# Seven products of quarters in place of eight: latent keys and six gate tiles of an attention encoder on one core

## The chip, the cores and the metric

The kernel runs on one core of a Trainium2 chip. A core has five engines with queues of their own: PE (matmuls; PEld is its weight load), DVE, ACT and POOL (elementwise work, of which POOL can't read the matmuls' accumulators in PSUM), and SP, which here only issues DMA transfers. The metric is device time in microseconds of one execution.

## The reference, cut to what matters

```python
def mla_mixer(h, w_in, q_norm, w_uq, kv_norm, w_ukv, w_out):
    proj = h @ w_in                       # h = rms_norm(x, g), 1024 x 1024
    c_q, c_kv, k_pe, gate = proj[..., :s1], proj[..., s1:s2], proj[..., s2:s3], proj[..., s3:]
    q = (rms_norm(c_q, q_norm) @ w_uq).reshape(B, L, MLA_HEADS, MLA_QK_DIM)
    kv = (rms_norm(c_kv, kv_norm) @ w_ukv).reshape(B, L, MLA_HEADS, QK_NOPE_DIM + V_HEAD_DIM)
    ...
    q_pe = apply_rope(q_pe, cos[:, None, :], sin[:, None, :])
    k_pe = apply_rope(k_pe, cos, sin)
    ...
    return (o * jax.nn.silu(gate)) @ w_out

h = x + mla_mixer(rms_norm(x, g), ...)    # DEPTH = 1: one layer
return rms_norm(h, final_norm)
```

With 1024 tokens and width 1024, `proj` has 384 columns of latent queries, 256 of latent keys and values ("latent keys" below), 64 of rotary key and 1024 of gate (8 heads of 128).

## The kernel before

All is float32, made from pairs: an operand is split into a high part of a shorter mantissa that PE multiplies fast and a low part (the rest), and `mm3` adds three products, high by high, high by low and low by high. `split` makes a high part on POOL and the low part on DVE. Activations lie transposed: `xh`, `xl` hold x times its gain, 8 blocks of 128 rows (k) by 1024 tokens. The norm's factor of each token (`rx`) is applied to results.

Stages, in the order of the program:

1. Latent queries (lines 161 to 192): for each k, x and a block of weights are loaded and split, and three output tiles of 128 x 1024 are accumulated, 144 matmuls of 512 columns. Copies put them into `craw[0]` to `craw[2]`.
2. The gate stage (lines 274 to 380). `stream(m)` computes one output tile of 128 x 1024: raw weights are loaded in two parts of 256 KB (`gwr`, two buffers), split into `gwh` and `gwl` (three buffers each), and 8 k by 2 halves by 3 make 48 matmuls. Tiles 3 and 4 are the latent keys, then come a rotary key (32 matmuls, lines 285 to 311), and eight gate tiles (`stream_gate`: a product with `rx_sb` on DVE, then Silu on ACT). `rstd_x` makes `rx` from rows of x; `latent_sums`, `latent_norm` and `latent_scale` normalise the latents; `cq_h`, `cq_l` are the split queries. Between gate tiles 1 to 4 `rope_half` computes rotary queries (18 matmuls a call), turns them with DVE, POOL and ACT in rooms of the home tiles (`craw_a`, `craw_b`) and sends the parts to a scratch tensor in memory, `qpe_d`.
3. Attention for 8 heads (lines 385 to 727), which reads `qpe_d` back, makes keys, queries and values of a head, scores, softmax, an exchange through DMA and the products with values; then the output projection and the last norm.

The order on each engine is planned when the program is built: the planner takes ready instructions by their place in the program's text (`later` moves that place), against a model of durations, and each engine then runs its list in order. A tile from a pool waits until the buffer's last reader is done; the pools of the gate stage close at line 382, and attention's pools take their memory.

Of the kernel before, what the change touches and what calls it, by code (L numbers as in the profile page):

```python
# [14 lines left out]
P = 128  # L15
# [14 lines left out]
def kernel(  # L30
# [19 lines left out]


    nc = tc.nc
    mm = nc.tensor.matmul

    def f32(ap):
        return ap.bitcast(F32)

    def mm3(ps, lh, ll, rh, rl, first, last):
        mm(ps, lhsT=lh, rhs=rh, start=first, stop=False)  # L59
        mm(ps, lhsT=lh, rhs=rl, start=False, stop=False)  # L60
        mm(ps, lhsT=ll, rhs=rh, start=False, stop=last)  # L61

# [55 lines left out]
    gp = xctx.enter_context(tc.tile_pool(name="gp", bufs=3, side="right"))  # L118
    rw = xctx.enter_context(tc.tile_pool(name="rw", bufs=2, side="right"))
    xp = xctx.enter_context(tc.tile_pool(name="xp", bufs=1, side="right"))  # L120
# [3 lines left out]
    def total(ssq, half, name):  # L124


        src = ssq[:, halves(half)]
        top = xs.tile([DR, HT], F32, name="ss_t")
        both = xs.tile([P, HT], F32R, name="ss_b")
        nc.scalar.copy(top, src[DR:P])  # L130
        nc.gpsimd.tensor_add(top, top, src[0:DR])
        nc.scalar.copy(both[0:DR], top)
        nc.vector.tensor_sub(both[DR:P], top, f32(both[0:DR]))
        ps = ps_t.tile([P, HT], F32, name=f"sum_{name}", tag="t")
        mm(ps, lhsT=ones, rhs=both, start=True, stop=True)
        return ps

    def rsqrt(v, s, r):
# [5 lines left out]
        nc.vector.scalar_tensor_tensor(r, s, 1.5, r, op0=ALU.add, op1=ALU.mult)  # L144

    with ExitStack() as wctx:
        wp = wctx.enter_context(tc.tile_pool(name="wp", bufs=3))

# [12 lines left out]
        for k in range(KD):  # L161
# [14 lines left out]
            for hs in [halves(0), halves(1)] if k < 3 else [slice(0, L)]:  # L176
                nc.scalar.activation(xh[:, k, hs], xr[:, hs], AF.Copy, scale=g_sb[:, k:k + 1])
                nc.vector.scalar_tensor_tensor(
                    xl[:, k, hs], xr[:, hs], g_sb[:, k:k + 1], f32(xh[:, k, hs]),
                    op0=ALU.mult, op1=ALU.subtract,  # L180
                )
            units = [(m, half) for half in range(2) for m in range(3)]
            if k == KD - 1:
# [9 lines left out]

    gpool = ctx.enter_context(tc.tile_pool(name="gate", bufs=1))
    gate = gpool.tile([P, H, L], F32, name="gate")
    cctx = ExitStack()
    wts = cctx.enter_context(tc.tile_pool(name="wts", bufs=1))
    kvp = cctx.enter_context(tc.tile_pool(name="kvp", bufs=1))
    kv_h = kvp.tile([P, 2, L], F32R, name="kv_h")
    kv_l = kvp.tile([P, 2, L], F32R, name="kv_l")  # L200
    rx_sb = xs.tile([P, L], F32, name="rx_sb")
# [10 lines left out]

    def rstd_x():

        rows = x.rearrange("(p j) c -> p j c", j=KD)
        for j in range(KD):
            xn = home[1][:, 1 + j % 3]
            nc.sync.dma_start(xn, rows[:, j])
            nc.scalar.activation(xn, xn, AF.Square, accum_out=ssx[:, j:j + 1])
        nc.vector.tensor_scalar(v_s, ssx, 1.0 / D, EPS, op0=ALU.mult, op1=ALU.add)  # L220
        rsqrt(v_s, s_s, rx)
        nc.vector.tensor_mul(mx, rx, rx)
        spread("rx", rx, rx_sb)

    def latent_sums(ms, name):
        cs, sq = gate[:, 4], gate[:, 5]
        for i, m in enumerate(ms):
            if i == 0:
                nc.scalar.activation(cs, craw[m], AF.Square)
            else:  # L230
                nc.scalar.activation(sq, craw[m], AF.Square)
                nc.gpsimd.tensor_add(cs, cs, sq)
        line = gate[0:1, 6]
# [17 lines left out]

    def stream(m):
        wh, wl = [], []
        for kq in range(2):
            wh.append(gp.tile([P, 4, P], F32R, name=f"gwh_{m}_{kq}", tag="gwh"))
            wl.append(gp.tile([P, 4, P], F32R, name=f"gwl_{m}_{kq}", tag="gwl"))
            wr = gp.tile([P, 4, P], F32, name=f"gwr_{m}_{kq}", tag="gwr", bufs=2)
            nc.sync.dma_start(wr, wg[m - 3 - (m > 5), :, kq * 4:(kq + 1) * 4])
            split(wr, wh[-1], wl[-1])
        ps = wide(f"g_{m}")  # L260
        for k in range(KD):
            for half in range(2):
                hs = halves(half)
                mm3(ps[:, hs], wh[k // 4][:, k % 4], wl[k // 4][:, k % 4], xh[:, k, hs], xl[:, k, hs],
                    k == 0, k == KD - 1)
        return ps

    def stream_gate(i):
        ps = stream(6 + i)
        gt = gate[:, i]  # L270
        nc.vector.tensor_mul(gt, ps, rx_sb)
        nc.scalar.activation(gt, gt, AF.Silu)

    rstd_x()
    ps = stream(3)
    nc.scalar.copy(craw[3], ps)
    latent_sums((0, 1, 2), "sq")
    ps = stream(4)
    nc.scalar.copy(craw[4], ps)
    latent_norm("sq", QR, "rq", gate[:, 7])  # L280
    latent_sums((3, 4), "sk")

    wr = gp.tile([P, KD, DR], F32, name="wpe_r", tag="gwr", bufs=2)
    nc.sync.dma_start(wr, wpe)
# [4 lines left out]
    for k in range(KD):  # L291
        w = w_pe[k // 4][:, k % 4].rearrange("p a b -> p (a b)")
        for half in range(2):
            hs = halves(half)
            mm(ps[:, hs], lhsT=w, rhs=xh[:, k, hs], start=k == 0, stop=False)
            mm(ps[:, hs], lhsT=w, rhs=xl[:, k, hs], start=False, stop=k == KD - 1)
    rk_sb = gate[0:DR, 1:3]
    nc.sync.dma_start(rk_sb, rope_k)
    kp = home[1][:, 3]
    nc.vector.tensor_mul(kp, ps, rx_sb)  # L300
    kr = gate[:, 3]
# [10 lines left out]

    latent_scale((0, 1, 2), gate[:, 7])
    latent_norm("sk", KR, "rk", gate[:, 7])
    cqp = cctx.enter_context(tc.tile_pool(name="cqp", bufs=1))
    cq_h = [cqp.tile([P, L], F32R, name=f"cq_h{m}") for m in range(3)]
    cq_l = [cqp.tile([P, L], F32R, name=f"cq_l{m}") for m in range(3)]
    for m in range(3):
        nc.scalar.copy(cq_h[m], craw[m])
        nc.vector.tensor_sub(cq_l[m], craw[m], f32(cq_h[m]))  # L320
    stream_gate(0)
    def load_split(shape, src, tag, bufs, pool=None, raw=None):
# [3 lines left out]
        wr = (raw or wts).tile(shape, F32, name=f"{tag}_r", tag="w_r")  # L326
        nc.sync.dma_start(wr, src)
        split(wr, wh, wl)
        return wh, wl

    def load_q(src, pool=None):
        return load_split([P, 3, P], src, "wq", 2, pool, pool)

    def load_k(h):
        return load_split([P, 2, P], wuk[h], "wk", 1)

# [4 lines left out]
    nc.sync.dma_start(rope_sb, rope_q.rearrange("c p t -> p c t"))  # L341
    rooms = [(home[0][:, 0], home[0][:, 1]), (home[0][:, 2], home[1][:, 3])]

    def rope_half(g, half, w):
# [3 lines left out]
        for i in range(2):  # L348
            ab.append(acc("ab"))
            for k in range(3):  # L350
                mm3(ab[i], w[i][0][:, k], w[i][1][:, k], cq_h[k][:, hs], cq_l[k][:, hs], k == 0, k == 2)
        cos, sin = rope_sb[:, 0, hs], rope_sb[:, 1, hs]
        for i, (f0, f1, op) in enumerate(((cos, sin, ALU.subtract), (sin, cos, ALU.add))):
            t, hl = rooms[((g * 2 + half) * 2 + i) % len(rooms)]
            t0, t1 = t[:, 0:HT], t[:, HT:L]
            hi, lo = hl[:, 0:HT], hl[:, HT:L]
            nc.vector.tensor_mul(t0, ab[0], f0)
            nc.vector.tensor_mul(t1, ab[1], f1)
            nc.gpsimd.tensor_tensor(t0, t0, t1, op=op)
            nc.scalar.copy(hi.bitcast(F32R), t0)  # L360
            nc.vector.tensor_sub(lo.bitcast(F32R), t0, hi)
            for c, src in ((i, hi), (2 + i, lo)):
                nc.sync.dma_start(qpe_d[g * 4:(g + 1) * 4, c, :, hs], src)

    w_rope = [[load_q(wqp[j], rw) for j in range(2)], None]
    for i in range(1, H):
        stream_gate(i)
        if i == 2:
            w_rope[1] = [load_q(wqp[2 + j]) for j in range(2)]
        if i == 5:  # L370
            latent_scale((3, 4), gate[:, 7])
        if i == 6:
            for m in range(2):
                nc.gpsimd.tensor_scalar(kv_h[:, m], craw[3 + m], 1.0, 1.0, op0=ALU.mult, op1=ALU.mult)
                nc.vector.tensor_sub(kv_l[:, m], craw[3 + m], f32(kv_h[:, m]))
# [430 lines left out]
```

## Time and profile before

| | |
|---|---|
| median of 3 runs | 587.53 us (587.33 to 588.08) |
| profiled execution | 587.4 us |
| its span, first to last instruction | 585.7 us |
| mean granted clock of PE | 0.993 |
| matmuls in the profile | 2604 |

The page gives for each engine its busy time, for slices of the span the busy share, and for groups of equal instructions the number, mean duration and what the engine waited for. Windows give the same for a chosen stretch; the timeline gives the single instructions with start and duration in us. Durations of matmuls overlap, so their spacing is read from starts.

### The profile page before, as it was taken

How to read it: one execution, taken by the hardware profiler on the slowest of the kernel's cores; microseconds unless marked ns; L12 is line 12 of the kernel's file. 1: busy time of each engine (PE TensorE's matmuls, PEld its weight loads, DVE VectorE, ACT ScalarE, POOL GpSimd, SP SyncE). 2: the span in 40 equal slices, each digit the busy share in tenths (PEclk: the TensorE clock that was granted, in tenths of full speed). 3: DMA queues.
4: the chain of work that ended last, by engine and by line, in shares of the span. 5: the costliest groups of instructions: out<-in, count | busy, mean ns of one | idle time of the engine just before them, and what ended most of it. 6: DMA issues, size and time to landing. Idle time of an engine off the chain costs nothing.

```text
span 585.7 us, 7657 instructions
## 1 busy us (share of the span) xinstructions
PE 571.8 (98%) x2604; PEld 472.8 (81%) x2604; DVE 425.4 (73%) x573; ACT 275.5 (47%) x438; POOL 233.8 (40%) x201
## 2 busy tenths in 40 slices
PE   9999999999999999999999999999999979999995
PEld 5888888888888878888888888888888858788885
DVE  4923589475236799988888988898888894984663
ACT  4348463021014455553655455645365662644652
POOL 1623512343102345643553535533434874683000
PEclk9999999999999999999999999999999979999999
DMA  8766221324211448674457464763476458521332
GB/s 263 275 206 245 95 74 38 124 93 141 109 38 46 94 117 193 154 171 109 107 132 179 105 153 109 168 148 94 100 162 147 132 135 213 198 77 54 138 132 107
DMA packets 35962, 78.66 MB, mean 134 GB/s; under 512 B 7314, under 2 KB 11154, under 8 KB 35860
## 3 DMA queue, kind: packets, MB, share of 16 engines
q1 hardware_dynamic: 34628, 76.21, 48.3%
q10 hardware_dynamic: 1296, 1.97, 0.9%
q8 instruction: 20, 0.33, 0.2%
q14 instruction: 18, 0.15, 0.1%
HBM read 36.19 MB, written 8.41 MB: 76 GB/s over the span
## 4 chain that ended last, share of the span: by engine, by line
PE 90%; SPq 3%; DVE 2%; ACT 1%; DMA 1%; issue 1%; POOL 0%; DVEq 0%; ACTq 0%; POOLq 0%
PE g L59 6%; PE g L61 6%; PE g L60 6%; PE o L59 5%; PE o L60 5%; PE o L61 5%; PE pv L60 5%; PE pv L59 5%; PE pv L61 5%; PE s L59 4%; PE s L60 4%; PE s L459 4%; PE s L61 4%; PE s L458 4%; SPq L481 3%; PE q L59 2%
## 5 line engine op out<-in xcount | busy, mean ns | idle before, releaser
L472 POOL TENSOR_SCALAR probs<-probs,rc 128x1024 f32<-128x1024 f32 x64 | 84.3, 1319 | 113.0 <-DVE rc L471 108.9
L466 ACT ACTIVATE probs<-s,nmx 128x1024 f32<-128x1024 f32 x64 | 71.6, 1118 | 113.3 <-DVE nmx L464 110.4
L473 DVE STREAM_TRANSPOSE probs<-probs 128x1024 f32<-128x1024 f32 x64 | 79.2, 1238 | 15.8 <-POOL probs L472 14.2
L464 DVE TENSOR_REDUCE nmx<-s 128x1 f32<-128x1024 f32 x64 | 76.0, 1207 | 3.8 <-PE s L459 3.7
L488 ACT CAST pt_h<-d 128x1024 fp32r<-128x1024 f32 x64 | 65.3, 1052 | 8.0 <-PE pv L61 4.9
L59 PE MATMUL g<-xh,gwh 128*128 128x512 f32 x160 | 62.2, 389 | 0.0
L60 PE MATMUL g<-xl,gwh 128*128 128x512 f32 x160 | 62.2, 389 | 0.0
L61 PE MATMUL g<-xh,gwl 128*128 128x512 f32 x160 | 62.2, 389 | 0.0
L493 POOL TENSOR_TENSOR pt_l<-d,pt_h 128x512 fp32r<-128x512 f32 x32 | 49.1, 1534 | 26.0 <-ACT pt_h L488 25.3
L60 PE MATMUL pv<-pt_l,v_h 128*128 128x512 f32 x128 | 50.3, 393 | 2.4 <-POOL pt_l L493 2.0
L59 PE MATMUL s<-k_h,q_h 128*128 128x512 f32 x128 | 50.2, 392 | 1.2 <-ACT probs L466 1.2
L490 DVE TENSOR_TENSOR pt_l<-d,pt_h 128x1024 fp32r<-128x1024 f32 x32 | 48.8, 1524 | 3.5 <-ACT pt_h L488 3.3
L59 PE MATMUL pv<-pt_h,v_h 128*128 128x512 f32 x128 | 50.1, 392 | 0.0
L60 PE MATMUL s<-k_l,q_h 128*128 128x512 f32 x128 | 49.9, 390 | 0.0
L61 PE MATMUL pv<-pt_h,v_l 128*128 128x512 f32 x128 | 49.9, 389 | 0.0
L61 PE MATMUL s<-k_h,q_l 128*128 128x512 f32 x128 | 49.9, 389 | 0.0
L458 PE MATMUL s<-kk_h,qpe 128*128 128x512 f32 x128 | 49.8, 389 | 0.0
L459 PE MATMUL s<-kk_l,qpe 128*128 128x512 f32 x128 | 49.8, 389 | 0.0
L59 PE MATMUL o<-woh,o_split 128*128 128x512 f32 (+1 forms) x118 | 45.8, 388 | 2.5 <-ACT o_split L575 2.5
L60 PE MATMUL o<-wol,o_split 128*128 128x512 f32 (+1 forms) x118 | 45.6, 386 | 0.0
L61 PE MATMUL o<-woh,o_split 128*128 128x512 f32 (+1 forms) x118 | 44.5, 383 | 0.0
L576 DVE TENSOR_TENSOR o_split<-gate,o_split 128x512 fp32r<-128x512 f32 (+2 forms) x48 | 32.5, 708 | 9.4 <-ACT o_split L575 9.3
(194 smaller groups left out, 1237.1 us busy)
## 6 DMA issues: line engine op xcount, KB each, us to landing
d<-probs SPq DMA_DIRECT2D x256, 128.0 KB
gwr<-in_wg SPq DMA_DIRECT2D x20, 256.0 KB
craw_b<-in_x SPq DMA_DIRECT2D x8, 512.0 KB
qpe<-qpe_d SPq DMA_DIRECT2D x16, 256.0 KB
wor<-in_wo SPq DMA_DIRECT2D x16, 256.0 KB
xr<-in_x SPq DMA_DIRECT2D x16, 256.0 KB
xr<-in_xT SPq DMA_DIRECT2D x5, 512.0 KB
qpe_d<-craw_a SPq DMA_DIRECT2D x8, 256.0 KB
```

The lines of the kernel that those rows point to most:

```text
L59: mm(ps, lhsT=lh, rhs=rh, start=first, stop=False)
L60: mm(ps, lhsT=lh, rhs=rl, start=False, stop=False)
L61: mm(ps, lhsT=ll, rhs=rh, start=False, stop=last)
L458: mm(s[:, ks], lhsT=qpe_s, rhs=kk_h[:, ks], start=False, stop=False)
L459: mm(s[:, ks], lhsT=qpe_s, rhs=kk_l[:, ks], start=False, stop=True)
L464: maxima[u] = nc.vector.tensor_reduce(nmx, s, axis=AX.X, op=ALU.max, negate=True)
L466: exps[u] = nc.scalar.activation(p_t.rearrange("p j k c -> p k j c"), s.rearrange("p (k j c) -> p k j c", k=8, j=4), AF.Exp, bias=nmx, acc ...
L472: nc.gpsimd.tensor_scalar(p_t, p_t, rc, 1.0, op0=ALU.mult, op1=ALU.mult)
L473: nc.vector.transpose(out=p_t, in_=p_t)
L488: nc.scalar.copy(hi, src)
L490: nc.vector.tensor_sub(lo, src, f32(hi))
L493: nc.gpsimd.tensor_sub(lo[:, 2:4], src[:, 2:4], f32(hi[:, 2:4]))
```

## The change

Each of four pairs of output tiles (latent keys 3 and 4; gates 0 and 4, 1 and 5, 2 and 6) becomes a product of two 2 x 2 matrices of quarters: weights of tile a and of tile b, each for k 0 to 3 and 4 to 7, against x's four quarters `x11`, `x12`, `x21`, `x22` (k half by token half). It is computed by seven products with sums of quarters in front and behind: `t1` to `t4` are four sums of x's quarters, made once and split (`combine_x`; the first differences in the loop of stage 1; `t3` is written over `x12`, which `restore_x12` loads and splits again afterwards), and each pair makes four sums of weights and seven sums of results on DVE (`pair_start`, `pair_end`). A product is 4 k by 3 = 12 matmuls.

High parts of the gate weights are made by ACT instead of POOL; the latent sums by DVE instead of POOL. Raw weights have seven buffers instead of two. Gates 3 and 7 are computed as before, each in two halves, between the four rotary products (`gate_half`), and the rotary parts lie in `gwr`'s buffers instead of the home tiles. The rotary key's product comes right after the start of the first pair and is copied out at once. Several helpers are placed behind a given instruction (`issue_after`).

```diff
+            if k < 4:
+                nc.vector.tensor_sub(raw_a[:, k], xr[:, halves(1)], xr[:, halves(0)])
+                split_gained(raw_a[:, k], k, t1)
...
+    def combine_x():
+        for k in range(4):
+            nc.vector.scalar_tensor_tensor(
+                raw_a[:, k], raw_a[:, k], g_sb[:, k:k + 1], f32(x22[0][:, k]), op0=ALU.mult, op1=ALU.subtract
+            )
+        nc.vector.tensor_sub(raw_a, raw_a, f32(x22[1]))
+        split_act(raw_a, t2)
+        nc.vector.tensor_add(raw_b, raw_a, f32(x11[0]))
+        nc.vector.tensor_add(raw_b, raw_b, f32(x11[1]))
+        split_act(raw_b, t3)
+        nc.vector.tensor_add(raw_a, raw_a, f32(x21[0]))
+        nc.vector.tensor_add(raw_a, raw_a, f32(x21[1]))
+        return split_act(raw_a, t4)
+
+    def g_parts(src, shape=(P, 4, P)):
+        wh = gp.tile(list(shape), F32R, name="gwh", tag="gwh")
+        wl = gp.tile(list(shape), F32R, name="gwl", tag="gwl")
+        split_act(src, (wh, wl))
+        return wh, wl
...
+    def pair_start(a, b, dst_a, dst_b):
+
+        r11, r12 = g_load(a, 0), g_load(a, 1)
+        ps = wide("g")
+        p1, p2 = ps[:, 0:HT], ps[:, HT:L]
+        product(p1, g_parts(r11), x11)
+        nc.scalar.copy(dst_a[:, 0:HT], p1)
+        product(p2, g_parts(r12), x21)
+        return a, b, dst_a, dst_b, r11, r12, p2
+
+    def pair_end(state):
+        a, b, dst_a, dst_b, r11, r12, p2 = state
+        (c11, c12), (c21, c22) = ((d[:, 0:HT], d[:, HT:L]) for d in (dst_a, dst_b))
+        r21, r22 = g_load(b, 0), g_load(b, 1)
+        s = gp.tile([P, 4, P], F32, name=f"gws_{a}", tag="gwr", bufs=7)
+        nc.vector.tensor_add(s, r21, r22)
+        p5 = acc("g")
+        product(p5, g_parts(s), t1)
+        nc.vector.tensor_sub(s, r11, s)
+        p6 = ps_t.tile([P, HT], F32, name="g", tag="t")
+        product(p6, g_parts(s), t2)
+        nc.vector.tensor_add(c12, p6, c11)
+        nc.vector.tensor_add(c11, p2, c11)
+        nc.vector.tensor_sub(r21, r21, r11)
+        p7 = acc("g")
+        middle = product(p7, g_parts(r21), t3)
+        added = nc.vector.tensor_add(c21, p7, c12)
+        nc.vector.tensor_add(c22, p5, c21)
+        nc.vector.tensor_add(c12, p5, c12)
+        nc.vector.tensor_add(s, r12, s)
+        p3 = ps_t.tile([P, HT], F32, name="g", tag="t")
+        product(p3, g_parts(s), x22)
+        nc.vector.tensor_add(c12, p3, c12)
+        p4 = acc("g")
+        last = product(p4, g_parts(r22), t4)
+        nc.vector.tensor_add(c21, p4, c21)
+        return middle, added, last
...
+    pairs = [gate_start(0)]
+    combined = combine_x()
+    pair_end(first)
+    squares_x()
+    with tc.issue_after(combined.ins):
+        norm_x()
+    pairs.append(gate_start(1))
+    bounds = pair_end(pairs[0])
+    with tc.issue_after(bounds[0].ins):
+        latent_sums((0, 1, 2), "sq")
+    gate_end(0)
+    pairs.append(gate_start(2))
...
+    restore_x12()
+    direct = {"raw": [g_load(5, j) for j in range(2)]}
+    w_rope = [load_q(None, load_early([P, 3, P], wqp[j])) for j in range(2)]
+    gate_half(3, 0, direct)
+    direct["raw"] = [g_load(9, j) for j in range(2)]
+    raw_rope = [load_early([P, 3, P], wqp[2 + j]) for j in range(2)]
...
+    rope_half(0, 0, w_rope)
+    gate_half(3, 1, direct)
+    rope_half(0, 1, w_rope)
+    w_rope = [load_q(None, raw) for raw in raw_rope]
+    gate_half(7, 0, direct)
+    w_k = load_k(0, load_early([P, 2, P], wuk[0]))
+    latent_scale((3, 4), gate[:, 7])
...
+    rope_half(1, 0, w_rope)
+    gate_half(7, 1, direct)
+    rope_half(1, 1, w_rope)
```

More of the change, by code (lines that the diff above doesn't have):

```diff
@@ L60, in mm3 @@
         mm(ps, lhsT=lh, rhs=rl, start=False, stop=False)
-        mm(ps, lhsT=ll, rhs=rh, start=False, stop=last)
+        return mm(ps, lhsT=ll, rhs=rh, start=False, stop=last)
     def split(raw, hi, lo):
@@ L192 @@
         nc.vector.tensor_copy(craw[2][:, HT:L], a_5)
[L194 to L200, printed above, removed]
+    t2, t4 = t_parts("t2", "t4")
     rx_sb = xs.tile([P, L], F32, name="rx_sb")
@@ L268, in stream_gate, with split_act @@
[L268 to L285, printed above, removed]
+    def split_act(src, hl):
+        hi, lo = hl
+        nc.scalar.copy(hi, src)
+        return nc.vector.tensor_sub(lo, src, f32(hi))
@@ new lines, in g_parts, with g_load, product @@
+    def g_parts(src, shape=(P, 4, P)):
[3 more added lines that the diff above has]
+        return wh, wl
+    def g_load(w, j):
+        raw = gp.tile([P, 4, P], F32, name=f"gwr_{w}_{j}", tag="gwr", bufs=7)
+        nc.sync.dma_start(raw, wg[w, :, 4 * j:4 * j + 4])
+        return raw
+    def product(ps, w, x_part):
+        for k in range(4):
+            last = mm3(ps, w[0][:, k], w[1][:, k], x_part[0][:, k], x_part[1][:, k], k == 0, k == 3)
+        return last
@@ new lines, in gate_end, with gate_start, restore_x12 @@
+    def gate_end(i):
+        for j in (i, 4 + i):
+            nc.vector.tensor_mul(gate[:, j], gate[:, j], rx_sb)
+            nc.scalar.activation(gate[:, j], gate[:, j], AF.Silu)
+    def gate_start(i):
+        return pair_start(2 + i, 6 + i, gate[:, i], gate[:, 4 + i])
+    def restore_x12():
+        for k in range(4):
+            raw = gp.tile([P, HT], F32, name=f"xr2_{k}", tag="gwr", bufs=7)
+            nc.sync.dma_start(raw, xT[k * P:(k + 1) * P, halves(1)])
+            split_gained(raw, k, x12)
@@ new lines, in gate_half @@
+    def gate_half(i, half, state):
+        if half == 0:
+            state[i] = wide("g"), [g_parts(raw) for raw in state.pop("raw")]
+        ps, w = state[i]
+        hs = halves(half)
+        for k in range(KD):
+            mm3(ps[:, hs], w[k // 4][0][:, k % 4], w[k // 4][1][:, k % 4], xh[:, k, hs], xl[:, k, hs],
+                k == 0, k == KD - 1)
+        if half:
+            nc.vector.tensor_mul(gate[:, i], ps, rx_sb)
+            nc.scalar.activation(gate[:, i], gate[:, i], AF.Silu)
@@ L286 @@
+    first = pair_start(0, 1, craw[3], craw[4])
+    wr = gp.tile([P, KD, DR], F32, name="wpe_r", tag="gwr", bufs=7)
     nc.sync.dma_start(wr, wpe)
@@ L311 @@
         nc.vector.tensor_sub(kk_l[d], kp[0:DR], f32(kk_h[0:DR]))
-    latent_scale((0, 1, 2), gate[:, 7])
+    latent_norm("sq", QR, "rq", home[1][:, 3])
+    bounds = pair_end(pairs[1])
+    with tc.issue_after(bounds[2].ins):
+        latent_sums((3, 4), "sk")
+    gate_end(1)
+    bounds = pair_end(pairs[2])
+    with tc.issue_after(bounds[1].ins):
+        latent_scale((0, 1, 2), home[1][:, 3])
     latent_norm("sk", KR, "rk", gate[:, 7])
+    gate_end(2)
+    tctx.close()
+    cctx = ExitStack()
     cqp = cctx.enter_context(tc.tile_pool(name="cqp", bufs=1))
@@ L348, in rope_half @@
         for i in range(2):
-            ab.append(acc("ab"))
+            ab.append(acc("ab") if half == 0 else ps_t.tile([P, HT], F32, name="ab", tag="t"))
             for k in range(3):
```

104 lines of the change are left out of this document (53 added, 51 removed).

## The prediction

> **What bounds the kernel now.** I read the page's busy shares, its slices and its chain first. In the slices each digit is a fortieth of the span.
>
> ```profile
> span 585.7 us, 7657 instructions
> PE 571.8 (98%) x2604; PEld 472.8 (81%) x2604; DVE 425.4 (73%) x573; ACT 275.5 (47%) x438; POOL 233.8 (40%) x201
> PE   9999999999999999999999999999999979999995
> DVE  4923589475236799988888988898888894984663
> PE 90%; SPq 3%; DVE 2%; ACT 1%; DMA 1%; issue 1%; POOL 0%; DVEq 0%; ACTq 0%; POOLq 0%
> ```
>
> TensorE (PE) is busy 98% of the span and holds 90% of the chain, so a matmul removed is time removed as long as nothing else makes PE wait. VectorE (DVE) is half free in slices 3 to 12, the gate stage, and nearly full afterwards. Next I read the windows of the gate stage, and the first matmul of it, of the stage after it and of the scores.
>
> ```profile
> 37.90:171.40 133.50, 133.50 (x590) 110.35 (x589) 69.95 (x94) 49.10 (x66) 41.56 (x37) 1.00 0.33 110
> 37.92 0.39 PE L59 MATMUL g<-xh,gwh 128*128 128x512 f32 x1
> 171.36 0.39 PE L59 MATMUL k<-kv_h,wk_h 128*128 128x512 f32 x1
> 179.62 0.39 PE L59 MATMUL s<-k_h,q_h 128*128 128x512 f32 x1
> ```
>
> The columns after the stretch are its length, then busy us (and instructions) of PE, weight loads, DVE, ACT and POOL, the granted clock, the DMA share and GB/s. PE has no gap in 133.5 us; 590 matmuls make 0.2263 us each (the 389 ns means of the page overlap). DVE works 70 us of these 133.5, ACT 49, POOL 42. In the slices PE stays at 9 or more through the stages on both sides.
>
> **The change, part by part.** *Matmuls.* A pair of output tiles took 2 x 48; now it takes 7 products of 4 x 3 = 84. Four pairs (latent keys, gates 0/4, 1/5, 2/6) save 48 matmuls: 48 x 0.2263 = 10.9 us. The two direct gates, the rotary key (32) and the rotary products (72) keep their count. That is the whole gain, and all of it lies on the path. The stage would end at 171.4 - 10.9 = 160.5.
>
> *What pays for it.* Almost every added operation is DVE's, so I price DVE by spacing, from start to start where operations follow one another:
>
> ```profile
> 118.20 1.28 DVE L357 TENSOR_TENSOR craw_a<-ab,craw_b 128x512 f32<-128x512 f32 x2
> 119.40 1.27 DVE L358 TENSOR_TENSOR craw_a<-ab,craw_b 128x512 f32<-128x512 f32 x2
> 85.39 3.48 DVE L320 TENSOR_TENSOR cq_l<-craw_a,cq_h 128x1024 fp32r<-128x1024 f32 x3
> 88.80 2.76 DVE L311 TENSOR_TENSOR kk_l<-craw_b,kk_h 64x1024 fp32r<-64x1024 f32 x2
> 25.86 1.15 ACT L177 ACTIVATE xh<-xr,g_sb 128x1024 fp32r<-128x1024 f32 x1 [2.51 <-DMA xr<-in_xT]
> 29.07 1.27 DVE L178 SCALAR_TENSOR_TENSOR xl<-xr,g_sb,xh 128x1024 fp32r<-128x1024 f32 x1
> 36.76 1.23 DVE L190 COPY craw_a<-s_b 128x1024 f32<-128x1024 f32 x1 [4.63 <-PE s_b L61]
> 38.12 0.69 DVE L192 COPY craw_a<-acc 128x512 f32<-128x512 f32 x1
> 56.11 0.42 DVE L65 TENSOR_TENSOR wpe<-wpe_r,wpe 128x256 fp32r<-128x256 f32 x1
> 55.63 0.17 DVE L143 TENSOR_TENSOR small<-small 128x8 f32<-128x8 f32 x1
> 55.83 0.17 DVE L144 SCALAR_TENSOR_TENSOR small<-small 128x8 f32<-128x8 f32 x1
> ```
>
> Two 512-wide operations take 1.20 us (118.20 to 119.40): 0.60 each. Three 1024-wide ones take 3.41: 1.14 each. A 2048-wide one, which the trace lacks, is then 0.60 + 3 x 0.54 = 2.22 by the same slope (its bounds: two of 1024, 2.28, and four times 0.54, 2.16). An operation that reads its predecessor's result starts after its end (55.63 to 55.83 for 0.17), so a dependent 512-wide one costs about 0.1 more.
>
> When is DVE free for it? ACT ends the last split of x at 27.0; DVE's part and the last weight then end near 28.8 (at 29.07 before it was behind rotary weights, which the change loads later). And when must DVE be done? The last product of the third gate pair follows 24 + 32 + 24 + 60 + 24 + 60 + 24 + 60 + 48 matmuls and 4 sums: 360 x 0.2263 = 81.5 after 37.9, at 119.4. DVE has 90.6 us. In front of that product it owes:
>
> - combining the quarters: 4 gained subtractions, 2.5, and 8 of 2048 elements, 17.8;
> - the PSUM copies of the first stage, 1.8, and the rotary key's weights, 0.7;
> - four pairs, each with 4 weight sums, 7 low parts and 7 result sums: 70 before that point (the last two come later), 42.0, and about 20 dependent ones, 2.0;
> - the first two gate ends, 4 x 1.14 = 4.6; the rotary key, 7 x 1.14 = 8.0;
> - latent sums, now DVE's own: 3 x 1.14 + 8 x 0.60 = 8.2; two norms of small operations, 2.4.
>
> Together 90.0 us in 90.6. Nothing is to spare: DVE becomes as tight as PE. The rest to 160.5 (41.1 us) is direct gates, two gate ends, latent scaling, their splits, the restored quarter, rotary products and small rest, about 42, of which 4 can come after the stage. That is full too. So the question is how much of a full stretch DVE idles. The nearest row is its fullest stretch in the gate stage:
>
> ```profile
> 78.80:101.60 22.80, 22.80 (x102) 18.89 (x101) 21.81 (x28) 13.06 (x14) 4.97 (x6) 1.00 0.12 37
> ```
>
> 21.81 of 22.80, 4.3% idle. Then 90.0 / 0.957 = 94.0 us, 3.4 more than there is: PE waits 3.4 us. Bounds: 0 (DVE never idle, or work such as the rotary key put off) and, at 10% idle, 9.4. I take 3.4, the row's value; the second part then runs 3.4 later with its own work and adds none.
>
> *What POOL gives up.* The splits of gate weights go from POOL to ACT, the latent sums from POOL to DVE.
>
> ```profile
> L64 POOL TENSOR_SCALAR gwh<-gwr 128x512 fp32r<-128x512 f32 x20 | 15.9, 796 | 44.2 <-DMA gwr<-in_wg 24.2 <-PE g L60 19.4 <-PE pe L296 0.4
> L232 POOL TENSOR_TENSOR gate<-gate 128x1024 f32<-128x1024 f32 x3 | 7.2, 2404 | 11.8 <-ACT gate L231 11.8
> L361 DVE TENSOR_TENSOR craw_a<-craw_a 128x512 fp32r<-128x512 f32 x4 | 4.0, 988 | 4.5 <-ACT craw_a L360 2.9 <-DMA qpe_d<-craw_a 1.5
> 100.31 0.68 DVE L361 TENSOR_TENSOR craw_a<-craw_a 128x512 fp32r<-128x512 f32 x1
> 98.38 0.62 ACT L360 CAST craw_a<-craw_a 128x512 fp32r<-128x512 f32 x1 [2.26 <-POOL craw_a L359]
> L177 ACT ACTIVATE xh<-xr,g_sb 128x512 fp32r<-128x512 f32 x6 | 4.2, 723 | 3.7 <-DMA xr<-in_xT 2.7 <-DMA g_sb<-in_gains 0.9
> L178 DVE SCALAR_TENSOR_TENSOR xl<-xr,g_sb,xh 128x512 fp32r<-128x512 f32 x6 | 4.9, 841 | 4.5 <-ACT xh L177 4.5
> ```
>
> POOL is no bound, so what it loses is worth nothing by itself; but DVE's L361 has a mean of 988 ns, with POOL at work beside it, and takes 0.68 us in the row where POOL rests, so a quieter POOL keeps my 0.60. ACT gains 7 high parts and one copy per pair (32 x 0.6 = 19 us) and 6 us of combining; with 49 before it is far from full, and its cost is the hop from sum to high part to low part, about 2 us a product. Three buffers of split weights let that run two products (5.4 us) ahead. If DVE's queue is longer than that, PE waits: this is where the 3.4 us would show. I count ACT's hop at nothing more.
>
> *First stage.* Four quarters get a difference and a split: DVE 4 x (0.60 + 0.84) = 5.8, ACT 4 x 0.72 = 2.9.
>
> ```profile
> 0.00:25.00 25.00, 23.63 (x95) 17.30 (x96) 16.93 (x22) 10.39 (x12) 11.68 (x17) 1.00 0.87 297
> ```
>
> DVE is free for 8.1 of these 25 us, waiting for x (the last columns of L177 and L178), and the rotary weights' splits leave. The bounds are 0 and the whole 5.8; I take 0.3, near 0, as the free time is longer than the work.
>
> *DMA and SP.* Seven buffers of raw weights, 256 KB each, take over what two did; loads are issued one pair ahead, x for the norm comes as before, and the stage's DMA share of 0.33 leaves room: nothing, unless x's rows block SP's queue ahead of weights (then DVE's hop is late, the same 3.4 us place).
>
> *The seam to attention.* Before, the last work of the stage was a gate; now it is a rotary half, whose parts lie in the gate weights' buffers, and attention's first tiles take over that memory.
>
> ```profile
> 171.56 1.23 DVE L271 TENSOR_TENSOR gate<-g,rx_sb 128x1024 f32<-128x1024 f32 x1 [7.80 <-PE g L61]
> 172.87 0.81 SPq L437 DMA_DIRECT2D qpe<-qpe_d  x2
> 173.79 0.57 ACT L419 CAST k_h<-k 128x512 fp32r<-128x512 f32 x1
> 143.44 2.55 POOL L359 TENSOR_TENSOR craw_a<-craw_a 128x512 f32<-128x512 f32 x2 [3.71 <-DVE craw_a L358]
> 147.17 2.52 SPq L363 DMA_DIRECT2D qpe_d<-craw_b  x2
> ```
>
> The load of qpe left as the last gate's reader ended (172.79), so such waits are real. A rotary half's tail is 1.2 (DVE) + 2.55 (POOL) + 0.6 (ACT) + 0.7 (DVE) + 2.5 (SP), about 7.5 us; keys and queries give PE 8.3 us (171.36 to 179.62) without needing the scores. If keys' parts wait for that tail, scores start up to 7.5 + 5.8 (the way from the first key part to the scores, 173.8 to 179.6) - 8.3 = 5 us late; if they lie elsewhere, 0. I take 1.5, nearer to 0, as only some tiles overlap.
>
> **Sum.** Against the profiled execution's 587.4 us (0.1 under the median of 587.53; its span is 585.7, and I hold the 1.7 around it constant): 587.4 - 10.9 + 3.4 + 0.3 + 1.5 = 581.7.
>
> **A rule against the change.** Where PE did wait in this run:
>
> ```profile
> 472.00:475.00 3.00, 1.43 (x5) 0.86 (x5) 3.00 (x5) 0.84 (x1) 2.03 (x2) 1.00 0.87 187
> 475.00:478.00 3.00, 1.14 (x3) 0.70 (x4) 3.00 (x6) 3.00 (x7) 0.88 (x1) 0.51 0.65 231
> 478.00:481.00 3.00, 3.00 (x9) 2.33 (x9) 3.00 (x3) 3.00 (x5) 3.00 (x3) 0.50 0.00 0
> 481.00:484.00 3.00, 3.00 (x13) 2.44 (x12) 3.00 (x4) 0.72 (x2) 3.00 (x2) 0.85 0.00 0
> ```
>
> With PE idle 1.6 of 3 us and then 1.9 of 3, the clock fell to half and came back within 9 us. That cost 3 x (0.49 + 0.50 + 0.15) = 3.4 us besides the gaps. The Trainium skill, "TensorE: Matmul & The Clock Gate", Part 1, states that a window of about 3.4 us without work halves the clock; here less than one unbroken window was enough, and the row decides.
>
> **Rivals.** *Nothing lost*: DVE's 90.0 us fit, the seam is hidden, 576.5 to 578. For it: 90.0 is under 90.6. Against it: no row shows DVE full for 90 us. *Gaps that bunch*: if DVE's debt falls on one place, say the first product after combining, PE stands over 2.5 us, the clock halves, 3.4 us more each time: 585 with one, 588.5 with two. For it: the rows above; against it: the debt builds up slowly over 14 products, in gaps under 1 us. *Slower, DVE as the bound of the pairs*: every product needs sum, high part and low part across two in-order engines, and a rotary-key or gate operation of 1.14 us in DVE's queue delays it. If DVE idles 13% there, 90.0 / 0.87 - 90.6 = 12.8, and the time is 587.4 - 10.9 + 12.8 + 1.8 = 591.1. It decides from 9.7% idle on, where 9.1 us of waiting and the 1.8 eat the 10.9. For it: DVE and ACT alternate on almost every operand. Against it: with a queue of ready work DVE idled 4.3%. That the change doesn't do what it says I leave out: the diff fixes the count of matmuls.
>
> **How the numbers follow.** Forecast (DVE idle 2 to 8%, about 579.5 to 586): 0.55. Nothing lost: 0.15. Bunched gaps: 0.15, of which a third stays under 586.3, a third lies within 0.2% of 587.5 and a third above. Slower by DVE: 0.12. The remaining 0.03 is a seam of 5 us atop the forecast's upper end, no change. A measurement of this kernel tells some 0.2% from no change, so faster means under 586.3 and slower over 588.7: 0.75, 0.08, 0.17. The range, 577 to 589, leaves out half of "nothing lost" and most of the slow cases.
>
> **What would show it.** Right: PE's count falls by 48, matmul spacing stays 0.226, DVE over 90% from 30 to 160 us, PE gaps under 1 us before the products of weight sums with DVE's low part as releaser, 3 to 4 us in all. Wrong: DVE under 80% with PE waiting for ACT or DMA; granted clock below 1.00 between 38 and 160; scores later than 11 us after the last rotary product; or no gap at all, if the planner finds DVE other cover.

## The result, and the profile after

The changed kernel takes 618.75 us (618.47 to 620.46) against 587.73 us for the kernel before in the same comparison (587.33 to 588.08): ratio 1.0534, 95% interval 1.0514 to 1.0555. The forecast was 581.7, with 589 as its upper end. The span of the profiled execution grew by 30.7 us, from 585.7 to 616.4. First the page after, its busy shares, slices and chain.

```profile
span 616.4 us, 7712 instructions
PE 569.5 (92%) x2556; PEld 467.4 (76%) x2556; DVE 484.7 (79%) x660; ACT 308.7 (50%) x488; POOL 204.8 (33%) x172
...
PE   9997999999920899999999999999999979899995
...
DVE  6989889897750488998898898887888986693653
...
PEclk9997999999956799999999999999999999999998
...
PE 61%; DVE 11%; DMA 10%; ACT 6%; SPq 5%; issue 4%; POOL 3%; ACTq 0%; POOLq 0%; DVEq 0%
```

PE's count fell by 48, from 2604 to 2556, as forecast. DVE is at 8 tenths or more from the second slice to the ninth; from 30 to 160 us it works 115.6 of 130 us, 89%, where the prediction had over 90%. But PE has a hole of its own in slices 12 to 14 (169 to 216 us) with a low clock, and a tenth of the chain is DMA, of which there was 1% before. The windows of the new kernel say how much lies where: the gate stage, the place of the dip in slice 4, and the way from the stage's last product to the first scores.

```profile
38.20:169.60 131.40, 126.13 (x541) 102.41 (x539) 113.12 (x159) 76.50 (x106) 8.91 (x9) 0.97 0.32 100
50.00:62.00 12.00, 8.32 (x27) 6.34 (x26) 10.86 (x16) 11.46 (x16) 0.00 (x0) 0.72 0.16 55
169.60:209.80 40.20, 13.46 (x44) 10.29 (x43) 12.82 (x19) 5.59 (x9) 7.04 (x8) 0.62 0.27 96
```

The stage is 1.8 us shorter than before (131.4 against 133.2), where 10.9 us of products are gone. The way from the stage's last product to the first scores is 40.2 us long; before it was 8.5 (171.1 to 179.6). So the seam alone costs 31.7 us, and that is the loss: from the first exponentials on, the attention takes nearly what it took before (402.4 against 400.6 us to the end of the span). The first exponentials before and after:

```profile
185.13 1.12 ACT L466 ACTIVATE probs<-s,nmx 128x1024 f32<-128x1024 f32 x1
```

```profile
214.01 1.12 ACT L599 ACTIVATE probs<-s,nmx 128x1024 f32<-128x1024 f32 x1 [2.12 <-DVE nmx L597]
```

PE's waits from 38 to 210 us of the changed kernel, in total, times and longest:

```profile
PE q L62 <- POOL wq_h L67: 15.7, 1, 15.7
PE k L62 <- DVE craw_b L484: 11.0, 1, 11.0
PE g L62 <- ACT gate L392: 3.7, 1, 3.7
PE g L64 <- DVE gwl L279: 1.2, 2, 0.7
```

The two long ones end in the first key and the first query product; these rows of its timeline, and the first scores:

```profile
180.97 0.77 PE L62 MATMUL k<-kv_h,wk_h 128*128 128x512 f32 x1 [11.02 <-DVE craw_b L484]
202.06 0.79 PE L62 MATMUL q<-cq_h,wq_h 128*128 128x512 f32 x1 [15.72 <-POOL wq_h L67]
209.81 0.40 PE L62 MATMUL s<-k_h,q_h 128*128 128x512 f32 x1
```

The releasers are DVE and POOL, but neither is busy: in the 40.2 us DVE works 12.8 and POOL 7.0. They wait too. POOL's two long waits from 160 to 205 us are for the first head's query and key weights:

```profile
POOL wq_h L67 <- DMA early<-in_wqn: 18.7, 1, 18.7
...
POOL wk_h L67 <- DMA early<-in_wuk: 13.2, 1, 13.2
```

POOL's split of the key weights, at 173.2, lies in its list ahead of its sums for the third rotary half, which follow at 174.8. DVE's remainder of these weights and its products for the last two halves come behind it, and PE's wait of 11.0 us ends with the last of those. The timeline of SP, which issues the transfers, shows why the weights are late:

```profile
152.69 10.01 SPq L489 DMA_DIRECT2D qpe_d<-ab  x6
162.80 1.73 SPq L454 DMA_DIRECT2D early<-in_wuk  x1
164.62 25.12 SPq L489 DMA_DIRECT2D qpe_d<-ab  x10
189.85 1.61 SPq L454 DMA_DIRECT2D early<-in_wqn  x1
202.63 0.81 SPq L570 DMA_DIRECT2D qpe<-qpe_d  x2
```

And the chain of waits has two long pieces of DMA in that stretch (start, us, what):

```profile
165.24 12.52 DMA qpe_d<-ab
189.85 11.47 DMA early<-in_wqn
```

SP is held from 152.7 to 191.5 by sixteen writes of rotary parts, 256 KB each, and by two loads for the first head, one behind the sixth write and one behind the last. Two windows of the same kernel, inside that stream, give the DMA share and the rate in the last two columns; the third line is the rate in the second window, in 40 slices.

```profile
153.00:169.60 16.60, 16.60 (x75) 13.70 (x73) 12.69 (x14) 3.98 (x5) 4.71 (x4) 1.00 0.26 86
170.00:189.00 19.00, 5.38 (x12) 3.80 (x12) 8.64 (x12) 3.32 (x5) 5.40 (x5) 0.64 0.26 92
...
GB/s 103 99 103 101 97 104 99 99 103 103 103 103 103 103 95 65 52 26 13 39 78 73 91 95 103 103 99 99 103 103 103 99 103 99 103 103 103 103 99 99
```

The DMA engines are busy for 0.26 of the time, as if a quarter of them worked and the rest stood. The writes flow at about 102 GB/s, with a dip near 178 us, for which the parts of the third rotary half came late. 16 x 262,144 bytes at 102 GB/s are 41 us; with the dip the stream lasts from 152.7 to some 200, and the load behind the last write lands at 201.3. The Trainium skill, "DMA: Bandwidth & Descriptors", section "Why a DMA increments its semaphore by 16 and not by 1", states that a transfer uses the largest number of engines, up to 16, that divides the slowest dimension on both sides; the scratch is written as 4 heads of 32 rows, so four of sixteen, and the share of 0.26 agrees. The same writes were in the kernel before, at about the same rate, but spread from 100.8 to about 150 under a full PE. A window of the kernel before over four of them:

```profile
145.00:150.00 5.00, 5.00 (x24) 4.14 (x23) 2.05 (x3) 1.01 (x2) 1.83 (x3) 1.00 0.26 102
```

### The profile page after: what moved, and what is told of

Same layout as the page of the kernel before. It is cut to its first block, busy times and chain, and to the rows that moved or that the text cites. A ratio compares the mean times of both kernels' runs of the same rounds, so it can differ in the third digit from the quotient of the medians.

```text
span 616.4 us, 7712 instructions
## 1 busy us (share of the span) xinstructions
PE 569.5 (92%) x2556; PEld 467.4 (76%) x2556; DVE 484.7 (79%) x660; ACT 308.7 (50%) x488; POOL 204.8 (33%) x172
## 4 chain that ended last, share of the span: by engine, by line
PE 61%; DVE 11%; DMA 10%; ACT 6%; SPq 5%; issue 4%; POOL 3%; ACTq 0%; POOLq 0%; DVEq 0%
SPq L614 4%; PE o L64 4%; PE o L63 4%; PE o L62 4%; PE pv L63 4%; PE pv L64 4%; PE pv L62 3%; PE s L62 3%; PE s L64 3%; PE s L592 3%; PE s L63 3%; PE s L591 3%; PE g L64 3%; PE g L62 3%; PE g L63 2%
## 5 line engine op out<-in xcount | busy, mean ns | idle before, releaser
L67 POOL TENSOR_SCALAR wq_h<-early 128x384 fp32r<-128x384 f32 x5 | 3.5, 709 | 126.4 <-PE g L64 93.3
L62 PE MATMUL g<-xh,gwh 128*128 128x512 f32 x96 | 38.7, 403 | 4.1 <-ACT gate L392 3.7
L63 PE MATMUL g<-xl,gwh 128*128 128x512 f32 x96 | 38.3, 399 | 0.0
```

## The experiments

Four theories of the 31.7 us stood at first. **W**: the stream of slow writes, which the change moves to the end of the stage, is the loss, and whatever needs its end or stands behind it is late. **B**: the rotary parts hold the ring's seven buffers, and the loads wait for those. **Q**: the first head's two loads stand behind the writes in SP's queue. **L**: the rotary work is late, whatever its transfers cost. The ratios below are to the kernel before on the same chip; versions that ran on different chips are compared by their times, which for the kernel before differ by 0.6 us at most between chips.

### Which part of the seam

e1: each write as four of 32 rows, one for each head.

```diff
-                nc.sync.dma_start(qpe_d[g * 4:(g + 1) * 4, c, :, hs], src)
+                for a in range(4):
+                    nc.sync.dma_start(qpe_d[g * 4 + a, c, :, hs], src[a * 32:(a + 1) * 32])
```

> The changed kernel with each rotary part written to the scratch tensor in four transfers of 32 rows x 512, one for each head, in place of one of 4 x 32 x 512. Theory W (a write runs on a quarter of the DMA engines, 2.5 us each at 102 GB/s, 16 of them make 41 us from 152.7 us on, and the first head's weights stand behind them): each part takes under 1.2 us, PE's two waits of 11.0 and 15.7 us shrink to under 4 together, time 587 to 593. Theory L (rotary products this late cost the same however they are written): 612 to 619.

607.03 us, ratio 1.0323 (1.0286 to 1.036): 11.7 us come back with nothing else touched. That is between the two ranges, 5 us under L's and 14 us over W's. The stream has a new limit, SP itself:

```profile
153.53 17.59 SPq L490 DMA_DIRECT2D qpe_d<-ab  x32
...
171.69 15.00 SPq L490 DMA_DIRECT2D qpe_d<-ab  x32
```

SP takes 0.42 us to issue one (median), 27 us for 64, most of the 33 us of these rows, and each transfer lands 1.6 to 1.8 us after its issue. The scores come at 197.7 instead of 209.8.

e2: the rotary parts in the home tiles, as before the change, so that the ring is free for loads. e3: the first head's raw key and query weights in buffers of their own, loaded ahead of the rotary work.

```diff
-    rooms = [home[0][:, 0], home[0][:, 1], home[0][:, 2], home[1][:, 3]]
+    rooms = [(home[0][:, 0], home[0][:, 1]), (home[0][:, 2], home[1][:, 3])]
...
-            hi, lo = (gp.tile([P, HT], F32, name="ab", tag="gwr", bufs=7) for _ in range(2))
+            hi, lo = hl[:, 0:HT], hl[:, HT:L]
...
+    raw_k = xs.tile([P, 2, P], F32, name="raw_k", tag="ss_t")
+    nc.sync.dma_start(raw_k, wuk[0])
...
-    w_k = load_k(0, load_early([P, 2, P], wuk[0]))
+    w_k = load_k(0, raw_k)
...
```

> The changed kernel with the rotary parts back in the home tiles, as before; all else of the change stays. Theory B (the parts hold the ring of seven raw-weight buffers, so the first head's key and query weights get a buffer only when writes have landed): both loads leave ahead of most writes, PE's waits shrink to under 6 us together, time 588 to 595. Theory W: the 16 writes still need 41 us and delay the first head's rotary queries and DVE's rooms; 596 to 606.

> The changed kernel with the first head's raw key and query weights in buffers of their own (those of the latent sums, free by then), loaded ahead of the rotary products. Theory Q (only the place of these two loads behind the writes costs): the wait for the query weights (15.7 us) goes, and most of the 11.0; time 588 to 595. Theory B/W (the parts' ring still holds ACT, DVE and the accumulators until writes land): the 15.7 goes, 6 to 11 us of the other stay, 598 to 606.

e2: 618.41 us, 1.0517 (1.0486 to 1.0548). e3: 618.23 us, 1.0514 (1.0477 to 1.0551). Neither moves the time, and both lie above every range that was named. In e2 the ring holds no part, and both loads left at 136.6 and 137.9 us, ahead of the first write at 154.4; so with writes this slow neither the buffers nor the order help, and B and Q fall. The first scores come 13.7 us earlier there, at 196.1, but DVE and ACT now wait for the writes to free the home tiles, the next head's key weights wait behind the writes (10.0 us), and the first exponentials come at 213.8, as in the changed kernel (214.0). In e3 the wait for the query weights is gone, and another has its place; its waits from 164 to 216:

```profile
POOL wv_h L67 <- DMA qpe_d<-ab: 23.6, 1, 23.6
ACT k_h L556 <- DMA qpe_d<-ab: 19.9, 1, 19.9
PEld v L62 <- POOL wv_h L67: 19.0, 1, 19.0
PE v L62 <- POOL wv_h L67: 18.5, 1, 18.5
```

A cast of keys does not read the rotary parts. It waits for a write to land because its output lies where the ring lay (with the parts out of the ring, in e20 and e23 below, the wait is gone): the ring is closed at the end of the stage, and the attention's tiles take its memory. This is the handover that the prediction named; call it **M**.

e4: the kernel before, its products whole, with gates 6 and 7 in halves and a rotary half behind each, so that only the place of the rotary work changes.

```diff
+            for k in range(KD):
+                mm3(ps[:, hs], wh[k // 4][:, k % 4], wl[k // 4][:, k % 4], xh[:, k, hs], xl[:, k, hs],
+                    k == 0, k == KD - 1)
+            rope_half(i - 6, half, w_rope[i - 6])
...
-            rope_half(g, half, w_rope[g])
+    half_gates(6)
+    half_gates(7)
```

> The kernel before, with gates 6 and 7 in halves and a rotary half after each of these halves (as late as in the change), parts in the home tiles, first head's weights loaded at the start as before; no products of quarters. Theory L (late rotary products cost by themselves): 600 to 615. Theories B and Q (lateness alone costs little, the shared ring and queue do): 587 to 592, with the 16 writes still 2.5 us each and ending at about 185 us behind the first scores.

602.48 us, 1.0246 (1.0216 to 1.0276). The late rotary work, with its slow writes, costs 14.3 us (against 588.14 beside it) in a kernel that has neither the quarters nor the rotary parts in the ring. That is in L's range, but W explains it as well; this kernel with fast writes was not run, and L's test is e10, in which the rotary work is as late and only the writes are faster.

### The writes at full width

e10: the scratch laid out as two groups of 4 x 128 rows, so that a write is 128 rows of 512; a read is then the 4 x 32 rows. e13: that and e3's early loads. e11: that and the rotary key's sums in two single accumulators instead of a double one. e12: e10's layout in the kernel before.

```diff
-    qpe_d = dram.tile([H, 4, 32, L], F32, name="qpe_d")
+    qpe_d = dram.tile([2, 4, P, L], F32, name="qpe_d")
...
-                nc.sync.dma_start(qpe_d[g * 4:(g + 1) * 4, c, :, hs], src)
+                nc.sync.dma_start(qpe_d[g, c, :, hs], src)
...
-    ps = wide("pe")
+    ps = [acc("pe") for _ in range(2)]
...
```

> The changed kernel with the scratch tensor laid out so that a rotary part is written as 128 rows of 512 (and a head's part read as 4 x 32 x 512); nothing else. Theory W (a write of 4 x 32 x 512 uses a quarter of the DMA engines and 16 of them fill 41 us): a write lands in under 1.5 us, the write stream ends with the last rotary half, PE's seam waits of 26.7 us and the half clock behind them go down to 2 to 8; time 588 to 596. Theory I (the queue's order and buffers matter more than the writes' speed): still over 600.

> The same, and the first head's raw key and query weights in buffers of their own, loaded ahead of the rotary products. With fast writes the place of these loads costs what a landing and a split take: W expects 1 to 4 us less than the rows alone. Q, that the place of these loads is what matters, expects over 8 less.

> The same, and the rotary key's sums in the two single accumulators instead of a double one, so that the second pair needs not wait for their copy (PE waited 3.7 us at 54.7 us, after which the clock was at half). If the copy behind ACT's queue is what held PE there: the wait falls under 1.5 us, the clock stays at 1.00, 4 to 6 us less than without. If the weights' parts, ready at 53.1, hold it too: 1 to 2 us less.

> The kernel before with that layout of the scratch tensor. Its writes end 20 us ahead of the seam and PE never waits for them: no change, 587 to 588.5, unless reading a head's parts as 4 x 32 x 512 makes attention late (then over 589).

e10: 600.76 us, 1.0223 (1.0206 to 1.024), 18 us less than the changed kernel, from the layout alone. L can't be the whole, then; but W's range, 588 to 596, was missed, and 600.76 is just over the 600 of theory I, in part because the layout makes the reads narrow (e16 below). e13: 603.63 us, 1.026 (1.0237 to 1.0282), a miss: the early loads give nothing here and cost 2.9. e11: 597.67 us, 1.0161 (1.0137 to 1.0186): the gap at the rotary key is gone, and the stage ends at 165.7 instead of 171.0. e12: 592.43 us, 1.0077 (1.0056 to 1.0097): the layout costs the kernel before 4.3 us, since the narrow shape has moved to the reads. Its DMA from 170 to 190 us, in 40 slices, shows the two reads at nearly the same rate, 98 GB/s at a share of 0.2:

```profile
DMA  0000000002123772222221000003700000750000
GB/s 0 0 0 0 0 0 0 0 0 45 66 106 103 228 246 82 98 98 98 98 99 64 9 0 0 16 0 39 215 8 0 0 0 15 163 215 0 0 0 0
```

e15 and e16 cut the read in four transfers of 32 rows, in the kernel before and in the changed one. e14 has all of these parts and rotary halves one gate half earlier; e19 has that earlier order alone, with the slow writes.

```diff
-        nc.sync.dma_start(f32(qpe), qpe_d[h // 4, :, rows, halves(half)])
+        for c in range(4):
+            nc.sync.dma_start(f32(qpe)[c * 32:(c + 1) * 32], qpe_d[h // 4, c, rows, halves(half)])
...
+    rope_half(0, 1, w_rope)
     gate_half(3, 1, direct)
-    rope_half(0, 1, w_rope)
-    gate_half(7, 0, direct)
...
     rope_half(1, 0, w_rope)
-    gate_half(7, 1, direct)
     rope_half(1, 1, w_rope)
+    gate_half(7, 0, direct)
+    gate_half(7, 1, direct)
```

> The kernel before with the scratch stored by rows and the read back in four transfers of 32 rows. If the 4 us that storing by rows cost the kernel before come from the one 4x32x512 read, they go: 587.3 to 589, ratio 1.000 to 1.002, first scores at about 179.6 and the first exponentials again at 185. If they come from something else of the layout: 591 to 593.

> The changed kernel with the scratch by rows and the read back in four transfers of 32 rows, nothing else. Theory W: some 4 us less than by rows with one read (600.8), as in the kernel before: 595 to 598, ratio 1.013 to 1.017. If the read isn't on the way to the scores here: 600 to 602.

> The changed kernel with the scratch stored by rows (each write 128x512), the read back cut in four transfers of 32 rows, the first head's raw key and query weights in buffers of their own, the rotary key's sums in single accumulators, and the rotary halves one gate half earlier, so that a gate tile in two halves stands behind the last of them. Theory W (the slow writes at the end of the stage and what queues behind them are the loss; the saved products are worth some 10 us less what VectorE owes): first scores at 174 to 177 us, time 581 to 586, ratio 0.990 to 0.998. If the seam costs as much whatever the transfers are (the late rotary work itself, or VectorE behind by a half at the end of the stage): scores at 179 to 181 or later as in the run by rows with single accumulators, 592 to 598.

> The changed kernel with the rotary halves one gate half earlier and nothing else; the writes are the slow 4x32x512 ones. Theory W: the 41 us of writes begin some 11 to 14 us earlier, so the scores move forward by about as much, to 196 to 200 us: time 605 to 610, ratio 1.029 to 1.038. If only the place of the last rotary half counts (it then has a gate half of 11 us to hide in): scores by 183, time below 595.

e15: 587.98 us, 1.0011 (0.9995 to 1.0027), the time of the kernel before. e16: 596.42 us, 1.0132 (1.0114 to 1.0149). So of the 31 us the shape of these transfers is 22.3 (618.75 to 596.42): 18.0 with the writes, 4.3 with the reads. e19: 619.63 us, 1.0536 (1.0518 to 1.0553), a miss of mine: the earlier order leaves the first rotary half where it was, so the stream begins at 153.5 instead of 152.7 and ends no earlier: the load behind the last write is issued at 190.8 (189.9 in the changed kernel). A stream bound by its own rate wasn't helped by earlier data behind its first piece. e14: 590.52 us, 1.0035 (1.0024 to 1.0047), between the 581 to 586 that W alone gave and the 592 to 598 of the other reading.

### What is left

e18 is e14 with the rotary halves where the change has them. Two theories of its remainder: M, above, and **V**, that DVE is behind at the end of the stage. e20 is e14 with the parts in the home tiles (e2's edit); e21 is e20 with four of the rotary subtractions on POOL.

> The kernel of e14 with the rotary halves where the change has them, so that nothing stands behind the last of them. If the earlier order is worth what it was made for: 593 to 596, some 3 to 5 us more than e14, scores at 179. If the handover of the memory is the bound: the last write lands as late in both, and it is within 1.5 us of e14.

> The kernel of e14 with the rotary parts back in the home tiles, so that the ring of gate-weight buffers, whose memory the attention's tiles take over, has no write to wait for. Theory M (the handover of that memory is what is left of the loss): the waits of the key casts and of the value weights on the write's landing (2.6 and 5.5 us in e14) go, the first scores come at 174 to 176 instead of 179.9, time 582 to 586.5, ratio 0.990 to 0.998. Theory V (VectorE is behind): scores at 178 to 180 with the first key remainders late, 588 to 591.

> The kernel of e20 with the four subtractions of the later two rotary halves on GpSimd instead of VectorE (2.4 us less on VectorE, some 5 us more on GpSimd, in a stretch in which GpSimd is busy for 7 of 15 us). Theory M: within 1.5 us of e20, either way, since neither engine then stands before the scores. Theory V: 2 to 3 us less than e20.

e18: 589.55 us (587.39 to 591.79), 1.0033 (1.0022 to 1.0044), within 1.5 us of e14, so the earlier order was worth nothing. e20: 591.94 us, 1.0071 (1.0059 to 1.0084), a miss. e21: 591.51 us, 1.007 (1.0056 to 1.0083): no gain, as M expected and V not, but M had failed in e20. In e20 the casts of keys wait for no write, but PE waits 5.3 us before the key products (1.0 in e14), for DVE to free the accumulators of the last rotary half. Why that half is later in e20 than in e14 isn't shown; two pairs of home tiles hold the parts of four halves there, and that may be it. So V and M had to be taken apart without moving work to another engine. e22 is e18 without the eight subtractions for the low parts (the high part is written twice); e23 is e22 with the parts in the home tiles; e24 is e18 with the two subtractions of the latent keys on POOL.

```diff
-            nc.vector.tensor_sub(lo.bitcast(F32R), t0, hi)
-            for c, src in ((i, hi), (2 + i, lo)):
+            for c, src in ((i, hi), (2 + i, hi)):
...
-            hi = gp.tile([P, HT], F32, name="ab", tag="gwr", bufs=7)
+            hi = t[:, HT:L]
```

> The kernel of e18 without the eight subtractions that make the low parts of the rotary queries (the high part is written in their place, by as many writes): some 4.8 to 6 us less on VectorE between 145 and 172, none of it moved to another engine, and a shorter chain to the last write. Theory V (VectorE is late at the end of the stage): the wait of 3.4 us before the key products shrinks to 2 or less, the first scores come 2 to 4 us earlier, 585.5 to 587.5. Theory M (the memory's handover alone): the wait before the key products stays, scores within 1.5 us of e18, 588.5 to 590.

> The kernel of e22 with the high parts in the home tiles instead of the ring, so that the attention's memory waits for no write. If both V and M hold, the casts of the keys follow their products at once, scores at 173 to 175, 582 to 585. If V alone is left: within 1 us of e22. If something else keeps the seam: 588 or more.

> The kernel of e18 with the two 128x1024 subtractions that make the low part of the latent keys on GpSimd instead of VectorE (2.3 us less on VectorE at 156 to 158, some 5 us more on GpSimd, which is idle from 155 to 161 there). Theory V: 1 to 2.5 us less than e18, 587 to 588.5. Theory M: within 1 us of it.

e22: 586.7 us, 0.9983 (0.9971 to 0.9995). e23: 584.81 us, 0.995 (0.9937 to 0.9963). e24: 590.77 us, 1.0048 (1.0035 to 1.0061), another miss. The waits of e18 at the seam, and behind them those of e23:

```profile
POOL wv_h L67 <- DMA qpe_d<-ab: 4.1, 1, 4.1
...
PE k L62 <- DVE craw_b L485: 3.4, 1, 3.4
ACT k_h L557 <- DMA qpe_d<-ab: 3.4, 1, 3.4
```

```profile
POOL wv_h L67 <- DVE wq_l L68: 1.6, 1, 1.6
PE k L62 <- DVE craw_b L485: 1.5, 1, 1.5
```

Without the subtractions PE's wait before the keys is 1.9 us shorter and the median 2.9 us (0.9 us between the traced executions, of which e18's is its fastest), while the two DMA waits stay (3.7 and 2.9 us in e22). That speaks for V, but this edit also shortens the chain to the last write and halves the parts' share of the ring, so DVE's work alone is worth at most that. With the memory free of the write the two DMA waits go, and another 1.9 us: the first exponentials come at 182.2 in both, the second at 183.3 in e23 and 184.3 in e22. So V and M both have a part. Moving work to POOL (e21, e24) gave nothing: in e24 POOL's two subtractions take 2.54 and 2.82 us, and its additions for a rotary half, on the same chain, stand behind them; PE gets a new wait of 1.5 us before a rotary product. No version of the change that does the whole computation beat the kernel before; the nearest is e18, 0.3% over it. The milestones, read from the traces in us (starts of the products and of the exponentials), sum up the path. The traced execution of e16 and of e18 is its fastest, so the last column, a median, lies above it:

| kernel | last product of the gate stage | first key product | first scores | first exponentials | traced execution | time |
|---|---|---|---|---|---|---|
| before | 171.1 | 171.4 | 179.6 | 185.1 | 587.4 | 587.73 |
| after | 169.6 | 181.0 | 209.8 | 214.0 | 618.5 | 618.75 |
| e10, writes of 128 rows | 171.3 | 174.7 | 189.0 | 197.5 | 600.9 | 600.76 |
| e16, reads too | 169.1 | 172.5 | 185.1 | 192.1 | 594.6 | 596.42 |
| e18, single accumulators and early loads too | 164.6 | 168.4 | 177.8 | 183.3 | 587.4 | 589.55 |
| e22, eight subtractions left out | 165.8 | 167.7 | 176.7 | 182.2 | 586.5 | 586.70 |
| e23, and memory free of the writes | 164.9 | 166.8 | 175.1 | 182.2 | 584.8 | 584.81 |

## Why the prediction was wrong

**The step that failed is the seam to attention**, put at 1.5 us with bounds of 0 and 5, together with "DMA and SP: nothing". The seam cost 31.7, of which e10 and e16 give 22.3 back by the shape of the transfers alone. One of the prediction's own signs of being wrong came with it: the scores are 40 us behind the last rotary product, where 11 was the limit. The prediction named the right place (parts in the gate weights' buffers, whose memory the attention takes over, a load of qpe behind them), but sized a single half's tail and in it read the 2.52 us that SP took to issue two writes as the time of the transfer. It never summed the sixteen: 4.2 MB at the 102 GB/s that the trace before shows is 41 us, some 10 for each half. What hid them before was 70 us of gate products behind the first of them; the change moves them behind the last 17 us of the stage. Under "DMA and SP" only the loads were counted, and not what stands behind the writes in SP's queue: the first head's two loads, for which POOL waited 13.2 and 18.7 us.

**The matmuls, 10.9 us**: right. The stage's matmuls fell from 588 to 540 at 0.2265 us each.

**DVE, 3.4 us**: near in size, incomplete in place. 540 x 0.2265 are 122.3; the changed stage takes 131.4, so 9.1 are lost, of which 6.3 belong to one place (below) and 2.8 to the rest. Of these the trace puts 1.2 down to DVE's low parts, in two gaps; the others aren't traced to it. In e18, without that place's gap, the stage takes 126.5, 4.2 more than its products. DVE is busy for 102.28 of the 112 us from 38 to 150 there, and wholly from 150 to 160:

```profile
38.00:150.00 112.00, 109.79 (x476) 88.73 (x476) 102.28 (x148) 73.48 (x104) 9.98 (x8) 1.00 0.35 109
150.00:160.00 10.00, 10.00 (x46) 8.29 (x45) 10.00 (x12) 3.05 (x4) 3.02 (x3) 1.00 0.35 131
```

From 28.8 to 119.4 us, the stretch that the prediction priced, DVE works 83.95 of 90.6 us in e18. That is 7.3% idle instead of 4.3%, for which the prediction's own rule gives 6.5 us, more than was lost; that the size came near is partly luck. Where the sum was incomplete: it let "4 us come after the stage" for nothing. In the kernel before DVE ended the stage with 17 us to spare (4.01 of 21.1 us busy from 150 to 171.1), and PE had no wait before the keys. Now its queue is full when the stage ends, and by e22 that is worth at most 2.9 us.

**ACT's hop at nothing, and "gaps that bunch"**: one gap came, but not from DVE's debt. ACT's timeline after:

```profile
50.92 1.89 ACT L278 CAST t_h<-gate 128x2048 fp32r<-128x2048 f32 x1
52.72 1.05 ACT L253 ACTIVATE craw_b<-craw_a 128x1024 f32<-128x1024 f32 x1
53.67 0.99 ACT L392 COPY gate<-pe 128x1024 f32<-128x1024 f32 x1
```

The rotary key's copy out of its double accumulator waits behind a 2048-wide cast and a square, and the next gate product needs that accumulator. PE stands 3.7 us, and then twelve matmuls take 5.2 us instead of 2.7, most of them 0.427 us apart, 2.5 us more, where the rival allowed 3.4. The Trainium skill, "TensorE: Matmul & The Clock Gate", Part 1, gives about 3.4 us without work as what halves the clock, and this gap agrees. It isn't a limit below which the clock is safe: in the prediction's rows of the kernel before, the longest gap at 474 to 477 us was 2.46 us, and the clock halved. Single accumulators (e11) shorten the gap to 1.0 us; the clock then stays at 1.00, and the time falls by 6.0 us against e13.

**First stage, 0.3, and POOL**: right. The first gate product came at 38.2 after and 37.9 before; in the stage PE never waits for POOL.

With the transfers mended the seam comes into the stated bounds: in e18 it is 13.2 us against 8.5 before, 4.7 instead of 1.5, near the upper bound of 5. "Some tiles overlap" was a guess; the first key parts and the value weights did (the waits of e3 and e18). Even so e18's traced execution is only 1.8 us ahead of the kernel before at the first scores and at the first exponentials, where the sum had 5.7, and it loses that lead: from the first exponentials on it takes 402.0 us against 400.6, and e23 400.8. What takes the 1.4 us isn't shown. Why e18's median lies 2.2 us above its fastest run, the profiled one, stays open.

## What to carry to other kernels

When a step moves, list its transfers with bytes and measured rate, add them up, and compare the sum with what is left of cover at the new place; the time that the queue needs to issue them isn't the time that they take. A transfer that is hidden can be much slower than it need be without any sign in the time, and its DMA share in the windows gives it away. And where one pool's memory goes to the next stage, ask which transfers still read it: here a cast and a weight split that have nothing to do with a write waited 19.9 and 23.6 us for one (e3).

## What the runs showed of the hardware

A write of 4 x 32 x 512 elements and one of 128 x 512 have the same bytes, but the first held the DMA engines' share at 0.26 and about 102 GB/s, and 16 of them cost the changed kernel 18 us; the reads of that shape ran at 98 GB/s, and cutting them in four gave another 4.3. In e18 the wide kind landed in 2.0 us each (median). SP needed 0.42 us (median, e1) to issue a transfer of 32 x 512. And POOL's subtraction of 128 x 1024 took 2.54 to 2.82 us, where DVE's took 1.21: giving POOL some of a full DVE's work brought nothing here (e21, e24), though POOL was busy for only 9.0 of the 22 us from 150 to 172 in e18.
